# Dropping the explicit activation-table preload from a prefix log-sum-exp kernel

## The chip, the cores and the metric

The kernel runs on one core of one Trainium2 chip. The metric is the device time of one execution in microseconds (us). Three runs of the kernel before gave 1269.79, 1270.76 and 1274.91 us; the median is 1270.76. The engines are called PE (matmul), PEld (its weight loads), DVE (vector), ACT (activation functions), POOL and SP; the last two issue the transfers here.

## The reference

The input is x with B, S, D = 4, 4096, 4128 in float32, drawn from a normal distribution. Along the second axis (time) a running log-sum-exp is taken:

```
out[:, 0, :] = x[:, 0, :]
for t in range(1, S):
    mx = np.maximum(out[:, t - 1, :], x[:, t, :])
    out[:, t, :] = mx + np.log(np.exp(out[:, t - 1, :] - mx) + np.exp(x[:, t, :] - mx))
```

So out[t] is the logarithm of the sum of exp(x) over all time steps up to t, for each batch and each of 4128 columns. 270.5 MB are read and as many written.

## The kernel before

The kernel computes exp(x), takes prefix sums over time with triangular matrices on PE, and takes the logarithm of the sums.

A tile is 256 consecutive time steps of one batch, all 4128 columns. Each of the 128 partitions holds two consecutive time steps (R = 2), 33 KB in one run. There are 4 x 16 = 64 tiles, in order of batch and time. A tile's input `xt` (float32, 128 x 8256) comes from a pool of five buffers; its exponentials `et` (float16) from a pool of two. The logarithms are written over `xt`, and the store goes from there, so an `xt` buffer is free for a new load when its store has ended.

The order of the work is written out by hand (`tc.manual_schedule()`, line 130). For each tile the main loop issues the load of x on SP's queue (line 135), one Exp over the whole tile on ACT (line 139), and then `scan` of the tile before: Exp runs one tile ahead of Ln.

`scan` splits the columns into four chunks of 1024 and a tail of 32. For a chunk, `head` sums in PSUM (`pt`) the even time steps with the triangular matrix `incl`, the odd ones with `excl`, and the running total of the batch with `last` and the `carry` of the tile before (line 97). Ln of that gives the even time steps (line 98). `second` adds the odd time steps with `ident` (line 104), after the first Ln has read `pt`; Ln of that gives the odd steps (line 105), and DVE copies the sums to `carry` (line 106). The heads run one chunk ahead of the seconds. The tail's two time steps are summed in `qt` and go through one Ln (line 124). Then POOL's queue issues the store (line 126). All matmuls are recorded under the helper's line 80.

A tile thus has on ACT one Exp and nine Ln, in the order Exp of tile k+1, nine Ln of tile k, Exp of tile k+2, and so on. At the very start and the very end two Exps and two blocks of Ln follow each other.

[...] In line 66 the kernel loads, once at the start, the set `natural_log_exp_and_others`, and it names no set anywhere else. ACT has 640 ACTIVATE instructions and this one table load.

Of the kernel before, what the change touches and what calls it, by code (L numbers as in the profile page):

```python
# [1 line left out]

# [4 lines left out]

FP32 = mybir.dt.float32
FP16 = mybir.dt.float16
ACT = mybir.ActivationFunctionType  # L10
P = 128
R = 2
CH = 1024
MM = 512


def _constants(nc, pool):


    def tri(base, name):  # L20
        t = pool.tile([P, P], FP16, name=name)
        nc.gpsimd.memset(t, 1.0)

        nc.gpsimd.affine_select(  # L24
            out=t, in_=t, pattern=[[1, P]], compare_op=mybir.AluOpType.is_ge,
            fill=0.0, base=base, channel_multiplier=-1,
        )
        return t

    def ones_where_zero(base, mult, step, name):  # L30
        t = pool.tile([P, P], FP16, name=name)
        nc.gpsimd.memset(t, 0.0)
        nc.gpsimd.affine_select(  # L33
            out=t, in_=t, pattern=[[step, P]], compare_op=mybir.AluOpType.not_equal,
            fill=1.0, base=base, channel_multiplier=mult,
        )
        return t

    return (
        tri(0, "incl"),  # L40
        tri(-1, "excl"),
        ones_where_zero(0, 1, -1, "ident"),
        ones_where_zero(-(P - 1), 1, 0, "last"),
    )


@with_exitstack
def kernel(
    ctx: ExitStack,
    tc: tile.TileContext,  # L50
    x: bass.AP,
    out: bass.AP,
):

    nc = tc.nc
    B, S, D = x.shape
    rows = P * R
    n_t = S // rows  # L60
    assert S % rows == 0
    n_main = D // CH
    tail = D - n_main * CH
    t0 = n_main * CH

    nc.scalar.preload_act_table_set("natural_log_exp_and_others")  # L66
    consts = ctx.enter_context(tc.tile_pool(name="consts", bufs=1))
    incl, excl, ident, last = _constants(nc, consts)

    xpool = ctx.enter_context(tc.tile_pool(name="xpool", bufs=5))  # L70
    epool = ctx.enter_context(tc.tile_pool(name="epool", bufs=2))
    cpool = ctx.enter_context(tc.tile_pool(name="cpool", bufs=1))
    pmain = ctx.enter_context(tc.tile_pool(name="pmain", bufs=3, space=bass.MemoryType.PSUM))
    ptail = ctx.enter_context(tc.tile_pool(name="ptail", bufs=2, space=bass.MemoryType.PSUM))

    carry = [cpool.tile([P, CH], FP16, name=f"carry{c}") for c in range(n_main)]
    carry_t = cpool.tile([P, tail], FP16, name="carry_t") if tail else None

    def mm(pt, w, rhs, start, stop):
        nc.tensor.matmul(pt, lhsT=w, rhs=rhs, start=start, stop=stop, skip_group_check=True)  # L80

    def scan(b, k, xt, et):
        first = k == 0

        def head(c):
            pt = pmain.tile([P, CH], FP32, name="pt")
            for s in range(0, CH, MM):
                o = pt[:, s:s + MM]
                seg = slice(c * CH + s, c * CH + s + MM)
                mm(o, incl, et[:, 0, seg], True, False)  # L90
            for s in range(0, CH, MM):
                o = pt[:, s:s + MM]
                seg = slice(c * CH + s, c * CH + s + MM)
                mm(o, excl, et[:, 1, seg], False, first)
            if not first:
                for s in range(0, CH, MM):
                    mm(pt[:, s:s + MM], last, carry[c][:, s:s + MM], False, True)
            nc.scalar.activation(xt[:, 0, c * CH:(c + 1) * CH], pt, ACT.Ln)  # L98
            return pt

        def second(c, pt):
            for s in range(0, CH, MM):
                seg = slice(c * CH + s, c * CH + s + MM)
                mm(pt[:, s:s + MM], ident, et[:, 1, seg], False, True)
            nc.scalar.activation(xt[:, 1, c * CH:(c + 1) * CH], pt, ACT.Ln)  # L105
            nc.vector.tensor_copy(carry[c], pt)  # L106

        prev = None
        for c in range(n_main):
            pt = head(c)  # L110
            if prev is not None:
                second(c - 1, prev)
            prev = pt
        if tail:
            qt = ptail.tile([P, R, tail], FP32, name="qt")
            seg = slice(t0, D)
            for j in range(R):
                mm(qt[:, j, :], incl, et[:, 0, seg], j == 0, False)
                mm(qt[:, j, :], incl if j else excl, et[:, 1, seg], False, first)
                if not first:  # L120
                    mm(qt[:, j, :], last, carry_t, False, True)
        second(n_main - 1, prev)
        if tail:
            nc.scalar.activation(xt[:, :, t0:D], qt, ACT.Ln)  # L124
            nc.vector.tensor_copy(carry_t, qt[:, 1, :])  # L125
        nc.gpsimd.dma_start(  # L126
            out=out[b, k * rows:(k + 1) * rows, :].rearrange("(p j) d -> p j d", j=R), in_=xt,
        )

    ctx.enter_context(tc.manual_schedule())  # L130
    work = [(b, k) for b in range(B) for k in range(n_t)]
    pending = None
    for b, k in work:
        xt = xpool.tile([P, R, D], FP32, name="xt")
        nc.sync.dma_start(  # L135
            out=xt, in_=x[b, k * rows:(k + 1) * rows, :].rearrange("(p j) d -> p j d", j=R),
        )
        et = epool.tile([P, R, D], FP16, name="et")
        nc.scalar.activation(et, xt, ACT.Exp)  # L139
        if pending is not None:  # L140
            scan(*pending)
        pending = (b, k, xt, et)
    scan(*pending)


# [1 line left out]
_INS = ['x']  # L147
_OUTS = [((4, 4096, 4128), 'float32')]


# [23 lines left out]
```

## Time and profile before

| | |
|---|---|
| median of three runs | 1270.76 us |
| the profiled execution's own time | 1269.79 us |
| its span in the profile | 1268.1 us |
| ACT busy | 948.6 us (75%) |
| PE busy | 606.9 us (48%) |
| DVE busy | 313.8 us (25%) |
| moved by DMA | 541.47 MB, mean 427 GB/s |
| load of a tile, issue to landing | 27.0 us (median) |
| store of a tile, issue to landing | 34.2 us (median) |

A line of the profile's groups names the source line, the engine, the operation, output and input with their shapes and types, how often it ran, then its busy time in us and the mean duration of one in ns, then the engine's idle time just before it and what ended that idle time ("<-"). In a timeline the columns are start and duration in us, engine, line, operation and count; brackets hold the idle time before and what ended it. The digits of the slices are tenths of busy time in 40 equal parts of the span.

### The profile page before, as it was taken

To read this page: it belongs to the slowest core of one execution; us is meant where nothing else is said; L and a number is where in the kernel's file an instruction comes from. 1 tells how busy PE (TensorE), PEld (TensorE's weight loads), DVE (VectorE), ACT (ScalarE), POOL (GpSimd) and SP (SyncE) were. 2 spreads that over 40 slices of the span, in tenths; PEclk is the share of its full clock that TensorE was granted. 3 is DMA by queue.
4 is the path that set the end of the run, shared out by engine and by line. 5 is a ranking of instruction groups with operands and counts; after the bars stand their busy time and mean duration, and the time that the engine had idled before them with its cause. 6 is when DMAs were issued, how large, how long until landed. Compare 5 with 4: busy or idle time off the path is not lost.

```text
span 1268.1 us, 6438 instructions
## 1 busy us (share of the span) xinstructions
PE 606.9 (48%) x2392; PEld 241.0 (19%) x2392; DVE 313.8 (25%) x320; ACT 948.6 (75%) x641; POOL 36.0 (3%) x76
## 2 busy tenths in 40 slices
PE   1565455454354453644535445455354453544533
PEld 0222122121121221211212112121121121211211
DVE  0333122231231222312223222132231222312213
ACT  5987777767777777687777877777777777687774
POOL 0000000000000000000000000000000000000000
PEclk9787687786777867778778777786876877777777
DMA  9999999999999999999999999999999999999996
GB/s 401 430 418 433 434 432 433 433 432 433 432 432 432 433 433 433 432 434 433 433 433 432 433 433 432 432 433 433 434 433 432 433 434 433 432 433 432 432 411 273
DMA packets 18463, 541.47 MB, mean 427 GB/s; under 512 B 2048, under 2 KB 2048, under 8 KB 2048
## 3 DMA queue, kind: packets, MB, share of 16 engines
q1 hardware_dynamic: 9216, 270.54, 49.6%
q0 software_dynamic: 9216, 270.54, 49.5%
q8 instruction: 18, 0.29, 0.1%
q14 instruction: 13, 0.11, 0.0%
HBM read 270.53 MB, written 270.53 MB: 427 GB/s over the span
## 4 chain that ended last, share of the span: by engine, by line
issue 89%; DMA 6%; POOL 2%; ACT 1%; PE 1%; DVE 0%; POOLq 0%; DVEq 0%; SPq 0%
DMA xt<-in_x_dram 3%; DMA out_dram<-xt 3%; POOL out_dram L126 2%; PE pt L80 1%; ACT xt L98 0%; ACT xt L105 0%; DVE carry L106 0%; POOLq L126 0%; DVEq L169 0%; DVE carry_t L125 0%; ACT et L139 0%; SPq L135 0%; DVEq L125 0%
## 5 line engine op out<-in xcount | busy, mean ns | idle before, releaser
L139 ACT ACTIVATE et<-xt 128x8256 f16<-128x8256 f32 x64 | 453.4, 7084 | 181.1 <-DMA xt<-in_x_dram 181.1
L106 DVE CAST carry<-pt 128x1024 f16<-128x1024 f32 x256 | 307.5, 1222 | 940.1 <-ACT xt L105 940.1
L80 PE MATMUL pt<-et,ident 128*128 128x512 f16 x512 | 197.3, 475 | 603.2 <-ACT xt L98 603.2
L98 ACT ACTIVATE xt<-pt 128x1024 f32<-128x1024 f32 x256 | 254.4, 1020 | 110.3 <-PE pt L80 109.8
L105 ACT ACTIVATE xt<-pt 128x1024 f32<-128x1024 f32 x256 | 255.0, 1026 | 11.6 <-PE pt L80 11.6
L80 PE MATMUL pt<-et,incl 128*128 128x512 f16 x512 | 192.4, 464 | 41.0 <-DVE carry L106 20.5
L80 PE MATMUL pt<-et,excl 128*128 128x512 f16 x512 | 185.8, 450 | 0.0
L80 PEld LDWEIGHTS <-ident 128*128 128x128 f16 x512 | 55.6, 109 | 682.8 <-issue 659.0
L80 PE MATMUL pt<-carry,last 128*128 128x512 f16 x480 | 167.0, 434 | 0.0
L80 PEld LDWEIGHTS <-incl 128*128 128x128 f16 x704 | 73.7, 111 | 153.0 <-issue 116.4
L80 PEld LDWEIGHTS <-excl 128*128 128x128 f16 x576 | 64.5, 112 | 96.2 <-issue 48.9
L80 PEld LDWEIGHTS <-last 128*128 128x128 f16 x600 | 63.4, 108 | 77.7 <-issue 36.8
L126 POOL DMA_DIRECT2D out_dram<-xt x64 | 34.2, 534 | 1216.6 <-ACT xt L124 1216.6
L80 PE MATMUL qt<-et,incl 128*128 128x32 f16 x192 | 17.8, 177 | 0.0
L124 ACT ACTIVATE xt<-qt 128x64 f32<-128x64 f32 x64 | 16.0, 250 | 0.0
L80 PE MATMUL qt<-carry_t,last 128*128 128x32 f16 x120 | 15.1, 176 | 0.0
L125 DVE CAST carry_t<-qt 128x32 f16<-128x32 f32 x64 | 11.6, 181 | 0.0
L80 PE MATMUL qt<-et,excl 128*128 128x32 f16 x64 | 11.3, 176 | 0.0
L66 ACT ACT_TABLE_LOAD x1 | 1.3, 1283 | 0.8 <-PEq L158 0.8
L24 POOL TENSOR_SCALAR_AFFINE_SELECT excl<-excl 128x128 f16<-128x128 f16 x1 | 0.3, 288 | 0.0
L33 POOL TENSOR_SCALAR_AFFINE_SELECT ident<-ident 128x128 f16<-128x128 f16 x1 | 0.3, 288 | 0.0
L33 POOL TENSOR_SCALAR_AFFINE_SELECT last<-last 128x128 f16<-128x128 f16 x1 | 0.3, 288 | 0.0
(9 smaller groups left out, 1.5 us busy)
## 6 DMA issues: line engine op xcount, KB each, us to landing
xt<-in_x_dram SPq DMA_DIRECT2D x64, 4128.0 KB, 27.0
out_dram<-xt POOLq DMA_DIRECT2D x64, 4128.0 KB, 34.2
```

The source lines that it names most:

```text
L24: nc.gpsimd.affine_select(out=t, in_=t, pattern=[[1, P]], compare_op=mybir.AluOpType.is_ge, fill=0.0, base=base, channel_multiplier=-1,)
L33: nc.gpsimd.affine_select(out=t, in_=t, pattern=[[step, P]], compare_op=mybir.AluOpType.not_equal, fill=1.0, base=base, channel_multiplier ...
L66: nc.scalar.preload_act_table_set("natural_log_exp_and_others")
L80: nc.tensor.matmul(pt, lhsT=w, rhs=rhs, start=start, stop=stop, skip_group_check=True)
L98: nc.scalar.activation(xt[:, 0, c * CH:(c + 1) * CH], pt, ACT.Ln)
L105: nc.scalar.activation(xt[:, 1, c * CH:(c + 1) * CH], pt, ACT.Ln)
L106: nc.vector.tensor_copy(carry[c], pt)
L124: nc.scalar.activation(xt[:, :, t0:D], qt, ACT.Ln)
L125: nc.vector.tensor_copy(carry_t, qt[:, 1, :])
L126: nc.gpsimd.dma_start(out=out[b, k * rows:(k + 1) * rows, :].rearrange("(p j) d -> p j d", j=R), in_=xt,)
L139: nc.scalar.activation(et, xt, ACT.Exp)
```

## The change

The explicit load of the table set is taken out. The source names no set any more, so the compiler places the loads itself, ahead of each activation whose function the set loaded before does not hold by its choice of sets.

```
-    nc.scalar.preload_act_table_set("natural_log_exp_and_others")
     consts = ctx.enter_context(tc.tile_pool(name="consts", bufs=1))
     incl, excl, ident, last = _constants(nc, consts)
```

In the built program ACT has 126 table loads in place of one: set number 0 ahead of an Exp that follows a Ln (and ahead of the first Exp), set number 5 ahead of the first Ln after an Exp. The set loaded by the kernel before has number 6. The 640 ACTIVATE instructions and the order of all other engines' instructions are the same.

More of the change, by code (lines that the diff above doesn't have):

```diff
@@ L64 @@
     t0 = n_main * CH
-    nc.scalar.preload_act_table_set("natural_log_exp_and_others")
     consts = ctx.enter_context(tc.tile_pool(name="consts", bufs=1))
```

## The prediction

> **What bounds the kernel now.** I read the profile's page first: the busy shares, the 40 slices, the costliest groups. Busy shares and slices:
>
> ```profile
> span 1268.1 us, 6438 instructions
> PE 606.9 (48%) x2392; PEld 241.0 (19%) x2392; DVE 313.8 (25%) x320; ACT 948.6 (75%) x641; POOL 36.0 (3%) x76
> ...
> DMA  9999999999999999999999999999999999999996
> GB/s 401 430 418 433 434 432 433 433 432 433 432 432 432 433 433 433 432 434 433 433 433 432 433 433 432 432 433 433 434 433 432 433 434 433 432 433 432 432 411 273
> ```
>
> The DMA engines are busy in every slice and move a flat 432 to 434 GB/s: the transfers set the pace. ACT is the busiest engine, at 75%. The groups say what it does, and that its largest idle time is ended by the load of x:
>
> ```profile
> L139 ACT ACTIVATE et<-xt 128x8256 f16<-128x8256 f32 x64 | 453.4, 7084 | 181.1 <-DMA xt<-in_x_dram 181.1
> L98 ACT ACTIVATE xt<-pt 128x1024 f32<-128x1024 f32 x256 | 254.4, 1020 | 110.3 <-PE pt L80 109.8
> L105 ACT ACTIVATE xt<-pt 128x1024 f32<-128x1024 f32 x256 | 255.0, 1026 | 11.6 <-PE pt L80 11.6
> L124 ACT ACTIVATE xt<-qt 128x64 f32<-128x64 f32 x64 | 16.0, 250 | 0.0
> L66 ACT ACT_TABLE_LOAD x1 | 1.3, 1283 | 0.8 <-PEq L158 0.8
> ```
>
> The last line is the operation the change multiplies: one table load of 1,283 ns, at the start. Then ACT's own timeline, one tile in the steady part (start, duration, in brackets the idle time before):
>
> ```profile
> 597.35 7.08 ACT L139 ACTIVATE et<-xt 128x8256 f16<-128x8256 f32 x1 [3.07 <-DMA xt<-in_x_dram]
> 604.34 1.92 ACT L98 ACTIVATE xt<-pt 128x1024 f32<-128x1024 f32 x2
> 606.44 1.02 ACT L105 ACTIVATE xt<-pt 128x1024 f32<-128x1024 f32 x1 [0.18 <-PE pt L80]
> 609.00 1.02 ACT L98 ACTIVATE xt<-pt 128x1024 f32<-128x1024 f32 x1 [1.53 <-PE pt L80]
> 609.92 1.02 ACT L105 ACTIVATE xt<-pt 128x1024 f32<-128x1024 f32 x1
> 611.37 1.02 ACT L98 ACTIVATE xt<-pt 128x1024 f32<-128x1024 f32 x1 [0.43 <-PE pt L80]
> 612.29 1.94 ACT L105 ACTIVATE xt<-pt 128x1024 f32<-128x1024 f32 x2
> 614.10 0.24 ACT L124 ACTIVATE xt<-qt 128x64 f32<-128x64 f32 x1
> 617.00 7.08 ACT L139 ACTIVATE et<-xt 128x8256 f16<-128x8256 f32 x1 [2.66 <-DMA xt<-in_x_dram]
> ```
>
> A tile takes 617.00 - 597.35 = 19.65 us. ACT needs 614.34 - 597.35 = 16.99 of it (its short waits for PE included); the other 2.66 it waits for the load. Those 2.66 us are the cover of everything ACT may be given.
>
> The total cover: from the second Exp (22.96) to the last (1226.47) are 62 tiles in 1203.5 us. Of L139's 181.1 us of waiting, 11.09 and 2.69 lie before the first two Exps, so 167.3 us of DMA waits lie in this stretch. **ACT's chain without them is 1036.2 us, 16.71 a tile; the cover is 167.3 us, 2.70 a tile.**
>
> **The change part by part.** One line goes, the one that loads at the start a table set holding both Exp and Ln. In the changed program's instruction order ACT has 126 table loads in place of 1: set 0 ahead of each Exp that follows a Ln, set 5 ahead of the first Ln after an Exp. A tile of the steady part gets two. Order and tiles on PE, DVE, POOL and SP stay; ACT issues no DMA, so no transfer moves in a queue. The first load still ends before 13.2, when the first tile lands. Each load without its own wait:
>
> - The load for Exp stands after L124's Ln and ahead of the Exp that holds the wait for x. It can run while x is still on its way, so the DMA wait hides it as far as it lasts.
> - The load for Ln stands between the Exp and L98's first Ln, where ACT had no idle time. A PE wait stands ahead of it, for a matmul done some 8 us before. Queued behind it are all nine Ln; PE's ident matmuls (603.2 us of waiting for L98), DVE's carry casts and POOL's store wait for these, and SP's load of five tiles later waits for that store. All move back by one load, and the next Exp wait shrinks by as much.
>
> The price of a switch. The load's record is 1.283 us. Around it: the Exp ends at 604.43 while the next Ln starts at 604.34, an overlap of 0.09 that a load between them breaks (L124 to Exp has none in a tile that waits for x). A load may also need time to start or to let the next instruction start; the trace shows none in use. From below this is 0, and a gain is excluded, as the load is added work on an in-order engine. Nearest row: L98 and L124 give (1020 - 250) / 960 = 0.802 ns an element, so an ACTIVATE has about 0.20 us that do not depend on size. Far rows above: 0.29 us from L124's end (614.34) to POOL's store (614.63), a hand-over between engines, once on each side of a load. I take half of the nearest row, 0.10 a load, because neighbouring ACTIVATEs overlap about half of theirs.
>
> Per tile: 2 x 1.283 + 0.09 + 2 x 0.10 = **2.86 us, against 2.70 of cover**. Over 62 tiles: 177.3 - 167.3 = **10.0 us late at the last Exp**. ACT then sets the pace, at 16.71 + 2.86 = 19.57 us a tile over the whole run, where it was 19.41. What is late next is nothing else: the loads land ahead of it.
>
> The end: from the last Exp to the end of the span are 41.6 us. One Ln load falls into them, +1.5. The last two stores, from 1243.23 to 1268.1, take 24.9 us; alone, two of 4.227 MB at 433 GB/s are 19.5. So a DMA with less behind it gives back 0 to 5.4; with ACT only a little late I take 1.5, which cancels the load.
>
> Sum: span 1268.1 + 10.0 = 1278.1. The profiled execution took 1269.79, 1.7 more than its span, so 1279.8 by its own time; the median of three, 1270.76, is 1.0 above it. **Forecast: 1281 us, 0.8% slower.**
>
> [...]
>
> **The rivals.**
>
> *Hidden loads: not slower.* If a load needs no start time, a tile gets 2 x 1.283 + 0.09 = 2.66, under the 2.70 of cover, and DMA stays the bound. What remains is the Ln load in the tail: 1270.8 + 1.5 = 1272. It decides below (2.70 - 0.09) / 2 = 1.30 us a load; up to (2.70 + 0.10 - 0.09) / 2 = 1.36 stays within 0.5%, as 62 x 0.10 is 6.2 us. For it: the flat 433 GB/s, and five x buffers that let a late ACT catch up. Against it: it leaves 0.02 us a load. A time clearly below before has no mechanism; the small chance is for scatter and a better end.
>
> *A switch costs twice its record.* If ACT must empty and refill for as long as the load itself, a tile gets 4 x 1.283 + 0.09 = 5.22, the run 62 x 5.22 - 167.3 = 156 us: 1428 us with the tail. For it: nothing in this trace excludes it. Against it: an Exp and the Ln behind it overlap, so this engine empties in a fraction of 0.2 us.
>
> *PE's clock.* The waits for PE inside the Ln block, 109.8 + 11.6 = 121.4 us or 1.9 a tile, depend on when PE leaves its slow pace: its matmuls stand 0.43 us apart at first and 0.22 later. The block's waits run from 0.86 to 2.65 us a tile. If the later Ln made every tile the worst, that adds 0.73 x 62 = 45 us, to 1326. Against it: tiles 2 to 5, with shorter pauses of PE (6.2 us in place of 9.4), waited 1.56 to 2.20, much like the rest, so the pause does not order the waits.
>
> **How the numbers follow.** The forecast's mechanism, ACT a little over its cover: 0.50. Hidden loads: 0.28 (0.24 of it within 0.5%, 0.04 below). Double price: 0.13. PE's clock: 0.09. The upper end of the price, 0.29 on each side, gives 2 x (1.283 + 0.58) = 3.73 a tile, 62 x 3.73 - 167.3 = 64 us, 1335. The range is 1268 to 1335: from the hidden case with scatter to that end, PE's case inside, the double price outside. About 0.5%, 6 us, is what a measurement of this kernel can tell from no change (its three runs lie 1269.79 to 1274.91). Faster 0.04, within 0.5% 0.24, slower 0.50 + 0.13 + 0.09 = 0.72.
>
> **What would show it.** 126 table loads of about 1.28 us, ACT busy up by some 160 us to 87%. Right: L139's idle time before it ended by DMA falls from 181.1 to a few us beyond the first two tiles, the gap between Exp's end and the first Ln's start is near 1.4 us, GB/s sinks by a digit or so, and Exps stand about 19.6 apart from the first tiles on. Hidden: steady Exps still 19.65 apart, with waits of some tenths for x. Double: 2.6 us between Exp and Ln, 22 us a tile, DMA at nine tenths or less. PE: L98's waits for PE well over 110. What would make it wrong is above all the start time of a load: each 0.1 us of it is 12.4 us of the result.

## The result, and the profile after

The changed kernel takes 1290.24 us (median; 1289.72 to 1290.60), the kernel before 1271.3 us in the same comparison. The ratio is 1.0144, with a 95% interval of 1.0122 to 1.0167: slower by 1.4%. The forecast was 1281 us, 0.8% slower; its range, 1268 to 1335, holds the result.

The profile's page of the changed kernel, head, busy shares and slices (line numbers are one lower than before):

```profile
span 1288.7 us, 6563 instructions
PE 624.2 (48%) x2392; PEld 246.8 (19%) x2392; DVE 313.8 (24%) x320; ACT 1117.1 (87%) x766; POOL 36.0 (3%) x76
...
DMA  9999999999999999999999999999999999999966
GB/s 407 417 415 431 433 419 429 433 422 428 434 432 429 423 426 429 422 434 428 426 426 433 424 431 431 434 432 430 427 432 424 426 435 429 432 421 432 430 299 263
...
L138 ACT ACTIVATE et<-xt 128x8256 f16<-128x8256 f32 x64 | 453.3, 7082 | 14.7 <-DMA xt<-in_x_dram 14.0
L97 ACT ACTIVATE xt<-pt 128x1024 f32<-128x1024 f32 x256 | 255.2, 1022 | 126.6 <-PE pt L79 125.8
L104 ACT ACTIVATE xt<-pt 128x1024 f32<-128x1024 f32 x256 | 254.9, 1026 | 11.7 <-PE pt L79 11.7
...
L138 ACT ACT_TABLE_LOAD x63 | 80.8, 1283 | 1.9 <-PEq L157 0.8
L97 ACT ACT_TABLE_LOAD x63 | 80.8, 1283 | 1.1
```

Four things are to be read here. There are 126 table loads of 1,283 ns each. The wait for x ahead of Exp fell from 181.1 to 14.0 us, which is all before the first two tiles: ACT sets the pace now. The transfer rate is no longer flat, while the row of DMA digits is still nearly all nines: these digits do not tell whether the transfers set the pace, the wait for x does. And a line that the prediction took as fixed has grown: the waits for PE, from 109.8 + 11.6 = 121.4 to 125.8 + 11.7 = 137.5 us.

ACT's timeline shows the price of a load and the new length of a tile. Columns: start, duration, then the instruction, in brackets the idle time before it.

```profile
594.50 7.08 ACT L138 ACTIVATE et<-xt 128x8256 f16<-128x8256 f32 x1
601.60 1.28 ACT L97 ACT_TABLE_LOAD   x1
602.90 1.94 ACT L97 ACTIVATE xt<-pt 128x1024 f32<-128x1024 f32 x2
605.02 1.02 ACT L104 ACTIVATE xt<-pt 128x1024 f32<-128x1024 f32 x1 [0.19 <-PE pt L79]
607.58 1.02 ACT L97 ACTIVATE xt<-pt 128x1024 f32<-128x1024 f32 x1 [1.54 <-PE pt L79]
608.50 1.02 ACT L104 ACTIVATE xt<-pt 128x1024 f32<-128x1024 f32 x1
610.46 1.02 ACT L97 ACTIVATE xt<-pt 128x1024 f32<-128x1024 f32 x1 [0.94 <-PE pt L79]
611.38 1.94 ACT L104 ACTIVATE xt<-pt 128x1024 f32<-128x1024 f32 x2
613.18 0.24 ACT L123 ACTIVATE xt<-qt 128x64 f32<-128x64 f32 x1
613.45 1.28 ACT L138 ACT_TABLE_LOAD   x1
614.74 7.08 ACT L138 ACTIVATE et<-xt 128x8256 f16<-128x8256 f32 x1
```

From Exp's start to the first Ln are 602.90 - 594.50 = 8.40 us, where there were 6.99: the load ahead of Ln costs 1.41. From the tail Ln's end (613.42) to the next Exp are 1.32. A tile thus gets 1.41 + 1.32 = 2.73 us of loads; over all tiles the mean is 2.74.

The whole difference of the two spans, 20.6 us, can be laid out from the two timelines, over the 62 tiles from the second Exp to the last:

| term | us |
|---|---|
| table loads, 62 x 2.74 | +169.7 |
| waits of the Ln block for PE, 1.90 to 2.17 a tile | +16.6 |
| waits for x, 167.3 to 0 | -167.3 |
| the rest (overlaps of neighbours) | +0.4 |
| first two Exps later | +0.2 |
| from the last Exp to the end, 41.6 to 42.6 | +1.0 |

The loads alone exceed the cover by 2.4 us. The waits for PE are seven times that. So the question is why PE, whose work and order did not change, makes ACT wait longer.

### The profile page after: what moved, and what is told of

It reads as the page before. It is cut to its first block, busy times and chain, and to the rows that moved or that the text cites. A ratio compares the mean times of both kernels' runs of the same rounds, so it can differ in the third digit from the quotient of the medians.

```text
span 1288.7 us, 6563 instructions
## 1 busy us (share of the span) xinstructions
PE 624.2 (48%) x2392; PEld 246.8 (19%) x2392; DVE 313.8 (24%) x320; ACT 1117.1 (87%) x766; POOL 36.0 (3%) x76
## 4 chain that ended last, share of the span: by engine, by line
ACT 60%; PE 35%; issue 2%; DMA 2%; DVE 0%; DVEq 0%; SPq 0%; ACTq 0%
PE pt L79 35%; ACT et L138 34%; ACT xt L97 11%; ACT L97 6%; ACT L138 6%; ACT xt L104 2%; DMA xt<-in_x_dram 2%; ACT xt L123 1%; DVE carry L105 0%; DVEq L168 0%; SPq L134 0%; DVE carry_t L124 0%; ACTq L97 0%; DVEq L124 0%
## 5 line engine op out<-in xcount | busy, mean ns | idle before, releaser
L79 PE MATMUL pt<-et,ident 128*128 128x512 f16 x512 | 202.2, 486 | 606.4 <-ACT xt L97 606.4
L138 ACT ACTIVATE et<-xt 128x8256 f16<-128x8256 f32 x64 | 453.3, 7082 | 14.7 <-DMA xt<-in_x_dram 14.0
L97 ACT ACTIVATE xt<-pt 128x1024 f32<-128x1024 f32 x256 | 255.2, 1022 | 126.6 <-PE pt L79 125.8
L104 ACT ACTIVATE xt<-pt 128x1024 f32<-128x1024 f32 x256 | 254.9, 1026 | 11.7 <-PE pt L79 11.7
L79 PE MATMUL pt<-et,incl 128*128 128x512 f16 x512 | 200.7, 482 | 41.2 <-DVE carry L105 20.7
L79 PE MATMUL pt<-et,excl 128*128 128x512 f16 x512 | 193.7, 468 | 0.0
L138 ACT ACT_TABLE_LOAD x63 | 80.8, 1283 | 1.9 <-PEq L157 0.8
L97 ACT ACT_TABLE_LOAD x63 | 80.8, 1283 | 1.1
L124 DVE CAST carry_t<-qt 128x32 f16<-128x32 f32 x64 | 11.6, 181 | 0.0
```

## Experiments

Two explanations were set against each other, besides the plain sum (each us on ACT's chain is a us of time, and the waits for PE are what they are). The *pause theory*: the load ahead of Ln lengthens PE's pause (its idle time in each tile ahead of the first `ident` matmul, which waits for the first Ln), and a longer pause makes its matmuls slower. The *clock-grid theory* comes from the windows of the changed kernel, cut here at steps of 3.413 us with a small gap between them (columns after the window: its length, busy time and count of PE, PEld, DVE, ACT and POOL, then the granted clock of PE, the share of DMA and GB/s):

```profile
602.92:606.28 3.36, 2.31 (x6) 0.86 (x6) 0.20 (x1) 2.94 (x3) 0.00 (x0) 0.50 0.95 413
606.34:609.69 3.35, 3.35 (x9) 1.22 (x8) 1.10 (x2) 1.94 (x2) 0.00 (x0) 0.50 0.98 424
609.75:613.10 3.35, 2.81 (x19) 1.35 (x18) 1.70 (x2) 2.64 (x3) 0.00 (x0) 1.00 1.03 444
613.16:616.52 3.36, 1.72 (x8) 0.58 (x6) 1.72 (x3) 3.33 (x4) 0.53 (x1) 1.00 1.08 457
616.58:619.93 3.35, 0.00 (x0) 0.00 (x0) 0.00 (x0) 3.35 (x1) 0.00 (x0) 1.00 1.02 434
619.99:623.34 3.35, 0.00 (x0) 0.00 (x0) 0.00 (x0) 3.32 (x3) 0.00 (x0) 0.50 0.87 355
623.40:626.76 3.36, 2.55 (x7) 0.90 (x7) 0.44 (x1) 2.70 (x3) 0.00 (x0) 0.50 1.07 462
626.82:630.17 3.35, 3.35 (x10) 1.15 (x9) 1.10 (x2) 1.94 (x2) 0.00 (x0) 0.50 1.05 453
630.23:633.58 3.35, 2.81 (x19) 1.35 (x18) 1.58 (x2) 2.76 (x4) 0.00 (x0) 1.00 1.03 444
```

Each step has one clock, 0.50 or 1.00. Cut at the same spacing from 16 to 1244 us, 360 steps in a row show the same: 187 at 1.00, 173 at 0.50, none between. So the steps run on evenly and do not follow the tiles. In the rows above the clock rises after a step in which PE was busy throughout (606.34 to 609.69) and falls after a step in which it did nothing (616.58 to 619.93). Elsewhere in the run 12 of its 61 rises stand behind a step with only 2.5 to 2.7 us of recorded matmuls and 13 of 61 falls behind one with 0.2 to 1.0 us, so what exactly makes the clock change stays open; the argument needs only the even steps. At 0.50 the matmuls of 512 columns stand 0.43 us apart in the trace, at 1.00 0.22. By these two figures a tile's burst of matmuls that starts 1 us earlier against the steps (an earlier *phase*) has 1 us more to go until the clock rises, does half as much in it, and, as an estimate, should make ACT wait 0.5 us longer.

Now six steps are 20.48 us. In the kernel before, DMA holds a tile at 19.65 us, 0.83 short of that, so each tile starts 0.83 us earlier against the steps than the one before, and its wait for PE grows by up to 0.42 until it slips by a whole step: 1.53, 1.72, 2.14 and 2.56 us in the tiles that start at 558.05, 577.69, 597.35 and 617.00. The waits for x make up the difference, 3.36, 3.07, 2.66 and 2.26 us at the ends of these tiles (brackets at the next Exp; the rows of 597.35 and 617.00 stand in the prediction):

```profile
558.05 7.08 ACT L139 ACTIVATE et<-xt 128x8256 f16<-128x8256 f32 x1 [2.19 <-DMA xt<-in_x_dram]
577.69 7.08 ACT L139 ACTIVATE et<-xt 128x8256 f16<-128x8256 f32 x1 [3.36 <-DMA xt<-in_x_dram]
636.66 7.08 ACT L139 ACTIVATE et<-xt 128x8256 f16<-128x8256 f32 x1 [2.26 <-DMA xt<-in_x_dram]
```

So the tiles go through the phases in even steps, about four tiles to a round. In the changed kernel nothing holds the tile; its length is 17.56 us of work plus the wait itself. These are the starts of Exp there (594.50 and 614.74, shown above, lie between the last two):

```profile
536.12 7.08 ACT L138 ACTIVATE et<-xt 128x8256 f16<-128x8256 f32 x1
554.95 7.08 ACT L138 ACTIVATE et<-xt 128x8256 f16<-128x8256 f32 x1
574.50 7.08 ACT L138 ACTIVATE et<-xt 128x8256 f16<-128x8256 f32 x1
635.10 7.08 ACT L138 ACTIVATE et<-xt 128x8256 f16<-128x8256 f32 x1
```

In the five tiles from 536.12 on the waits are 1.37, 1.96, 2.44, 2.67, 2.79 us and the lengths 18.83, 19.55, 20.00, 20.24, 20.36: what is missing to 20.48 about halves with each tile (1.65, 0.93, 0.48, 0.24, 0.12; their sum is one step), so the tiles gather where the wait is long. The mean of the five waits is 2.25 us; of the four above it is 1.99.

The pause theory does not fit the same five tiles. The brackets hold PE's pause:

```profile
545.58 1.01 PE L79 MATMUL pt<-et,ident 128*128 128x512 f16 x2 [9.05 <-ACT xt L97]
564.42 1.01 PE L79 MATMUL pt<-et,ident 128*128 128x512 f16 x2 [9.05 <-ACT xt L97]
583.96 1.01 PE L79 MATMUL pt<-et,ident 128*128 128x512 f16 x2 [9.05 <-ACT xt L97]
603.97 1.01 PE L79 MATMUL pt<-et,ident 128*128 128x512 f16 x2 [9.05 <-ACT xt L97]
624.21 1.01 PE L79 MATMUL pt<-et,ident 128*128 128x512 f16 x2 [9.05 <-ACT xt L97]
```

The pause is the same while the wait doubles from 1.37 to 2.79. And it hardly grew: it is 9.06 us on average over the run, where the kernel before has 9.00.

If the clock-grid theory is right, it has strange consequences that a plain sum cannot give, and the runs below look for them.

**One load, under the cover.** The kernel before with one load more in a tile.

```
         if pending is not None:
+            nc.scalar.preload_act_table_set("natural_log_exp_and_others")
             scan(*pending)
```

> The kernel before with one more table load, of the same set, ahead of the first Ln after each Exp: 63 added loads, none ahead of Exp. ACT's chain grows by about 1.41 us a tile, under the 2.70 us of cover. Clock-grid theory (waits for PE follow only from where a tile's burst falls on a fixed grid of 3.41 us at which PE's clock changes): the DMA keeps the pace at 19.65 us a tile, so the phase goes on by even steps, the waits for PE stay at about 118 to 122 us in all as in the kernel before, DMA waits of L139 fall from 181 to about 95 us, and the time is 1270 to 1274 us. Rival, pause theory (the load ahead of Ln lengthens PE's pause, and the longer pause makes its waits longer): waits for PE rise to about 137 us as in the changed kernel, still hidden.

Measured: 1271.37 us, ratio 1.0006 (0.9990 to 1.0022); all ratios here are to the kernel before, measured beside the run. The profile's waits of ACT:

```profile
ACT xt L98 <- PE pt L80: 112.8, 98, 1.5
ACT et L139 <- DMA xt<-in_x_dram: 89.7, 56, 11.3
ACT xt L105 <- PE pt L80: 11.7, 63, 0.2
```

The load is there, ahead of the first Ln, and costs nothing that can be told; the wait for x gives it up, 181.1 to 89.7. The waits for PE are 124.5 us, a little over the range given and far from the 137.5 of the changed kernel. The run was meant to set the pause theory against the other and cannot, for the load did not lengthen PE's pause: it is 8.96 us on average. What it shows is that the same load at the same place leaves PE's waits near the old ones where DMA still holds the pace, as it does in most tiles here. The pause theory falls by the rows above and by the third load below.

**Two loads of the same set.** The kernel before with both loads of the changed kernel, but each loads the set that is already there.

```
+    done = []
...
+        if len(done) > 1:
+            nc.scalar.preload_act_table_set("natural_log_exp_and_others")
+        done.append(k)
         nc.scalar.activation(et, xt, ACT.Exp)
         if pending is not None:
+            nc.scalar.preload_act_table_set("natural_log_exp_and_others")
             scan(*pending)
```

> The kernel before with a load of its one set ahead of each Exp and ahead of the first Ln after each Exp: 126 loads at the changed kernel's places, but no change of set. If a load costs the same whatever it loads: 1288 to 1292 us, like the changed kernel, PE waits of 134 to 140 us. Rival, that a switch to another set is what costs (or Ln and Exp run slower from the sets 5 and 0): clearly less, down to the 1271 of before.

Measured: 1290.27 us, ratio 1.0150 (1.0135 to 1.0165), waits for PE 125.8 + 11.7 = 137.5 us. It is the changed kernel again, to a tenth of a us. So the load instruction is the cause; that the sets differ, and which sets Exp and Ln run from, does not show.

**A third load.** One more, ahead of the tail's Ln, on top of the two.

```
+            nc.scalar.preload_act_table_set("natural_log_exp_and_others")
             nc.scalar.activation(xt[:, :, t0:D], qt, ACT.Ln)
```

> The kernel before with three table loads a tile: ahead of Exp, ahead of the first Ln, and ahead of the tail's Ln. By ACT's rows the third adds 1.283 + 0.04 + 0.10 (the overlap that it breaks) = 1.42 us a tile to the changed kernel's chain. Plain sum (every us on ACT's chain is a us, waits for PE as in the changed kernel): 62 x 1.42 = 88 us more than 1290, about 1378 us. Clock-grid theory: PE's clock changes only at steps of 3.413 us, a tile that gets shorter or longer moves against that grid, and its wait for PE moves by half of that the other way; so with 17.56 + 1.42 = 18.98 us of work ACT waits just long enough to make the tile 6 x 3.413 = 20.48 us: nearly all tiles 20.48 apart, waits of about 1.5 us a tile in place of 2.2, time 1335 to 1342 us.

Measured: 1340.48 us, ratio 1.0551 (1.0538 to 1.0565). The plain sum, 1378, falls. The starts of Exp in ACT's timeline, from a stretch inside the third batch:

```profile
903.34 7.08 ACT L144 ACTIVATE et<-xt 128x8256 f16<-128x8256 f32 x1
923.82 7.08 ACT L144 ACTIVATE et<-xt 128x8256 f16<-128x8256 f32 x1
944.30 7.08 ACT L144 ACTIVATE et<-xt 128x8256 f16<-128x8256 f32 x1
964.78 7.08 ACT L144 ACTIVATE et<-xt 128x8256 f16<-128x8256 f32 x1
```

Each tile takes 20.48 us, six steps, to the hundredth. The waits for PE fell to 88.6 + 11.7 = 100.3 us, 1.59 in a settled tile: work of 18.89 us plus just the wait that fills the six steps. PE's pause is 10.47 us in these tiles, 1.4 more than in the changed kernel, and the waits are shorter: the opposite of what the pause theory asks for. (The third load costs 18.89 - 17.56 = 1.33, not the 1.42 expected.)

**A quarter of a microsecond.** The changed kernel with a small ACTIVATE ahead of each Exp.

```
+    pad_in = consts.tile([P, 160], FP32, name="pad_in")
+    nc.vector.memset(pad_in, 0.0)
+    pad_out = consts.tile([P, 160], FP16, name="pad_out")
...
+        nc.scalar.activation(pad_out, pad_in, ACT.Exp)
         nc.scalar.activation(et, xt, ACT.Exp)
```

> The changed kernel with one small ACTIVATE (128 x 160, into a tile that nobody reads) ahead of each Exp: by ACT's rows 0.09 + 0.83 x 0.160 = 0.23 us a tile more. Plain sum: 62 x 0.23 = 14 us, about 1304 us. Clock-grid theory: 17.78 us of work can now wait its way up to 20.48 (2.7 us of waiting, which lies within what the tiles show), so most tiles settle at 20.48 after a batch's first tile has disturbed them; time 1318 to 1328 us, more than twice the plain sum's growth, with waits for PE of 2.4 us a tile or more.

Measured: 1323.99 us, ratio 1.0426 (1.0411 to 1.0441). Some 0.23 us of work a tile, 14 us in all, made the kernel 34 us slower. The waits for PE rose to 144.1 + 11.7 = 155.8 us, and the tiles settle at the same length as with the third load:

```profile
588.58 7.07 ACT L142 ACTIVATE et<-xt 128x8256 f16<-128x8256 f32 x1
609.06 7.07 ACT L142 ACTIVATE et<-xt 128x8256 f16<-128x8256 f32 x1
629.54 7.07 ACT L142 ACTIVATE et<-xt 128x8256 f16<-128x8256 f32 x1
650.02 7.07 ACT L142 ACTIVATE et<-xt 128x8256 f16<-128x8256 f32 x1
```

The settled waits are 0.19 + 1.54 + 0.95 = 2.68 us, so this is 17.80 us of work, against 18.89 with the third load, and both tiles take 20.48. The first tile of a batch, which has fewer matmuls, disturbs it and some eight tiles settle again; with the pad they do so from below (19.3, 19.42, 19.9, 20.19 us and so on), with the third load from above (20.73, 20.61), which is nearly all of the difference between the two runs.

**PE kept busy.** The changed kernel, and the kernel before, with 32 matmuls a tile into a PSUM bank that nobody reads, put into PE's pause. In the same edit the pool of `qt` goes from two buffers to one; the profiles list no wait for `qt`.

```
-    ptail = ctx.enter_context(tc.tile_pool(name="ptail", bufs=2, space=bass.MemoryType.PSUM))
+    ptail = ctx.enter_context(tc.tile_pool(name="ptail", bufs=1, space=bass.MemoryType.PSUM))
+
+    pwarm = ctx.enter_context(tc.tile_pool(name="pwarm", bufs=1, space=bass.MemoryType.PSUM))
+    wt = pwarm.tile([P, MM], FP32, name="wt")
...
             pt = head(c)
+            if c == 1:
+                for _ in range(32):
+                    mm(wt, incl, et[:, 0, 0:MM], True, True)
```

> The changed kernel with 32 further matmuls a tile on PE, into a PSUM bank nobody reads, after the second chunk's head and ahead of the first ident matmul, so that PE does not pause for long and its clock stays up. Both loads stay. Theory that the waits for PE are what takes ACT over its cover: waits for PE fall to about 0.9 us a tile (55 us), ACT needs 17.56 + 0.9 = 18.5 us a tile, under the 19.41 of the DMA, waits for x come back to some 40 to 70 us, time 1269 to 1274 us. Rival, that the loads themselves exceed the cover (2.86 us or more against 2.70): 1280 to 1290 us with hardly any wait for x.

> The kernel before with the same 32 further matmuls a tile. If the DMA alone sets its pace: waits for x on ACT grow by about what the waits for PE lose (some 60 us, from 181 to about 240), time 1269 to 1272 us, at most 2 us less by the shorter last Ln block. Rival, that the chain of ACT and PE has a share in its time: 1255 to 1265 us.

Measured: 1282.84 us for the changed kernel (ratio 1.0088, 1.0070 to 1.0106) and 1283.60 for the kernel before (1.0100, 1.0081 to 1.0118). Both times were missed, but the two are now alike: with PE's clock mostly up (0.94 and 0.93 in place of 0.76) the 125 loads more cost nothing that can be told. The waits of ACT in the changed kernel with the matmuls:

```profile
ACT xt L100 <- PE pt L82: 83.5, 89, 1.5
ACT et L144 <- DMA xt<-in_x_dram: 54.1, 43, 11.1
ACT xt L107 <- PE pt L82: 8.5, 13, 6.3
```

The waits for PE are 92.0 us in place of 137.5 (the expectation was 55; the granted clock is 0.94 on average, so it still falls at times), and x is waited for again, 54.1 us. Both times are some 12 us over the expectation. In both runs 6.3 us of that is one wait (the last line above has it; the other run's is as long) in the very last block, where the extra matmuls stand in the way with nothing to hide them. For the kernel before, whose ACT waits for x in nearly every tile of this run too, the rest is the DMA: without the matmuls it moves 433 GB/s in each of the windows 100 to 400, 400 to 700 and 700 to 1000 us, with them 432, 428 and 430, and the last Exp starts 10.6 us later (1237.11 for 1226.47). What slows the transfers was not tried. In the changed kernel with the matmuls the waits for PE, higher than expected, can have a part as well.

**The same, but not in the last block.**

```
-            if c == 1:
+            if c == 1 and not (b == B - 1 and k == n_t - 1):
```

> The changed kernel with the 32 further matmuls, left out in the very last block, where they stood in the way (6.3 us of waiting in the run before). Theory that ACT is back under its cover: 1275 to 1279 us, some 6 us under the run with all of them, and faster than the changed kernel although PE has 2016 more matmuls. Rival, that the run before was quicker by chance of phase alone: 1282 to 1290.

Measured: 1277.2 us, ratio 1.0058 (1.0045 to 1.0071), where the changed kernel has 1.0144 (1.0122 to 1.0167). PE does 2016 matmuls more, about 84% on top of its 2392, and the kernel is 13 us faster. The waits for PE are down to 84.2 + 2.4 = 86.6 us, and ACT waits for x again, 51.3 us: with these waits lower, both loads fit under the cover. The 7 us that remain over the kernel before (1270.33 us in this comparison) were not taken apart.

**The end.** The kernel before with the last two tiles stored in halves.

```
+                if ends and c == 2:
+                    store(0, 2 * CH)
...
+        if ends:
+            store(2 * CH, D)
+        else:
+            store(0, D)
```

> The kernel before with the last two tiles stored in two column halves each, the first as soon as its logarithms are there. The end (41.6 us from the last Exp to the end of the span) has DMA slices of 411 and 273 GB/s where it moves 433 elsewhere. If the late stores cost this: 3 to 7 us less, 1264 to 1268 us. Rival, that smaller runs and one more issue give it back: 1270 to 1272 us.

Measured: 1268.24 us, ratio 0.9988 (0.9974 to 1.0002). The median is 2 us lower, less than expected, and the interval holds 1. Ten of the twelve runs lie below the fastest of the seventeen of the kernel before (1269.34), two at 1273.55 and 1274.74: whether this is a gain stays open. No run is clearly faster than the kernel before.

## Why the prediction was right or wrong

*ACT becomes the bound, by a little: right.* L138's wait for x is gone, ACT is busy 87%, and the first load of the two is hidden as far as the wait for x lasts. The cover of 167.3 us was used up to the last. The sign that Exps stand about 19.6 us apart did not come: they stand 18.3 to 20.4 apart, 19.73 on average.

*The price of a load: a little high.* The sum took 2.86 us a tile; it measured 2.74, so 7.6 us too much over 62 tiles. Of the 0.10 us a load taken for starting, half the row of the fixed part of an ACTIVATE, about 0.04 is there: 0.02 before and 0.02 after a load in the timeline above. The rival of a double price falls: Exp's end to the Ln behind the load is 1.32 us, not 2.6, and one load's record of 1,283 ns is nearly all of it.

*The waits for PE taken as they were: wrong, and this is the term that decided.* The prediction put ACT's chain at 16.71 us a tile with the waits for PE in it as a constant 1.9. They rose to 2.17, 16.6 us in all. With the measured price and the old waits the sum would have been 2.4 us at the last Exp and about 3.6 at the end, no difference that can be told. That is the rival of hidden loads: the prediction let it reach up to 1.36 us a load, and measured were (2.74 - 0.09) / 2 = 1.33. That the forecast came out on the right side, at somewhat over half of the slowdown, is in good part luck: a load price that was too high stood in for the missing term.

*PE's clock as a rival: the right place, the wrong cause.* It was priced at the worst wait in every tile (45 us) through a longer pause of PE. The pause did not lengthen: 9.06 us on average for 9.00, and the same 9.05 in tiles that wait 1.37 and 2.79 us. One load under the cover raised the waits hardly (124.5 for 121.4 us). What raised them in the changed kernel is that the tile's length was no longer held by the DMA but by ACT, and with it by the waits themselves. The argument against the rival, that tiles 2 to 5 with shorter pauses waited no less, was sound against the pause and silent on the phase.

*The end: right in sum.* One load more and a give-back were to cancel; 1.0 us was left.

*"Each 0.1 us is 12.4 us of the result": wrong.* 0.23 us a tile cost 34 us where the plain sum has 14, and about 1.1 us more, the step from the pad to the third load, cost 16 where it has 68.

## What to carry to other kernels

Slack on an engine can be spent while something steadier holds the pace, and one load in a tile cost nothing that can be told here (1271.37 us, ratio 1.0006). When the slack is just used up, look at what else the pace was holding still: waits that depend on phase were an average over all phases before (1.90 us a tile here), and after the change the tile picks its own (2.17). A mean wait read from a trace is not a constant of the kernel.

## What the runs showed of the hardware that was not expected

In the changed kernel PE's clock changed only at steps of 3.413 us (360 in a row, each at 0.50 or 1.00), which did not follow the tiles. This loop, whose tiles PE's slow start can lengthen, settled on a multiple of them: tiles of 17.80 and of 18.89 us of work both took 20.48 us, six steps. The clock fell 61 times in the 360 steps, about once a tile, and that was no small matter here: 0.23 us of added work on ACT a tile cost 2.6% (1323.99 us for 1290.24), about half of it through longer waits for PE (155.8 us for 137.5).

A table load of the set that was already loaded cost as much as that of another one (1290.27 and 1290.24 us in all; 1.28 us a load in both traces).

The flat rate of the DMA in the kernel before, 433 GB/s, fell to 428 to 432 when PE was kept busy with matmuls that touch no DRAM. The cause is open.
